# Output projection of a hybrid decoder step: column tiles 0 to 3 and 12 to 15 with tokens as rows, the sample tokens in fp32 column groups, and only block 1 finished behind the last product

## The chip, the cores and the metric

The kernel runs on one core of one Trainium2 chip. The time is the device time of one execution, in microseconds (us). The program works in fp32 throughout; large products are made of float32r pieces.

## The reference, cut to what matters

One layer of a decoder is run on 512 prompt tokens and on 8 x 4 = 32 sample tokens. The part that the change touches is the end of it:

```python
y = (jax.nn.sigmoid(g_m) * jnp.einsum('btc,cd->btd', br_m, w_proj_m)
     + jax.nn.sigmoid(g_a) * jnp.einsum('btc,cd->btd', br_a, w_proj_a))
out = jnp.einsum('btc,cd->btd', y, w_out)
return _layernorm(DN_ALPHA * x + out, ln_w, ln_b).astype(x.dtype)
```

`y` and `x` have 2048 columns, `w_out` is 2048 x 2048. The layer norm runs over the 2048 columns of each token, so no token can be finished before the last column of its row is there.

## The kernel before, in words

**Layout.** Activations lie with features on the 128 partitions and T = 544 tokens (512 prompt, 32 sample) in the free dimension: 16 tiles of 128 features (index k). A weight column tile (index ct, 128 output columns) is loaded in two halves of 8 k each (`load_half`, 512 KB, three buffers of tag "raw") and split into a float32r high part and a low rest (`split`: ScalarE casts, VectorE subtracts). Each fp32 product is made of three float32r products: high x high, high x low, low x high. In `products` the weights are held in the array and the tokens move, 272 columns at a time.

**The output projection (`wo`) has four stages.**

- *Lead*, ct 0 to 3: `gemm` with all 544 tokens as moving columns, 96 products a tile. ScalarE copies the two banks into a tile, and SyncE's queue (SP) stores it to DRAM (`d_o`). Meanwhile `operand_sums` makes the sums for the next stage from reloaded `d_y`; it is a generator that `tick()` moves on, four ticks a tile.
- *Pairs*, ct 4 to 11: `paired` makes two column tiles with seven half products instead of eight (Strassen's scheme), each 24 matmuls of 272 columns. The results are parked in `d_o` too (`end_park`). `plain_back` reloads the lead's four tiles and hands them to `add_residual`: four PE transposes turn the prompt tokens into rows, VectorE adds them to the residual rows (`z0`, `zr`), and a fifth transpose does the samples, whose rows lie in `zs` with the four column quarters on four groups of 32 partitions.
- *Last four tiles*: ct 12 is again done with all tokens moving. For ct 13 to 15 the split weights are kept (`w3`), and only tokens 256 to 543 are done that way (288 moving columns). Then `rows_of(0)` and `rows_of(1)` do blocks 0 and 1 (128 tokens each) with the tokens held and 384 weight columns moving, so their result already has tokens as rows. During these tiles `pairs_back` transposes the eight parked tiles, `load_rows` brings the residual rows, `fetch` the parked tiles and `load_ln` the norm's weights, all through SP.
- *End*: blocks 2 and 3 and the samples are normalised during the row products (`others`, `finish`, `moments`). Block 0's sum and weighting also run there (`first_rows`), but its bias is added on PE behind the last product (`scaled`, with `biases`). Block 1 follows whole: `add_rows`, statistics, four quarters `weighed` on VectorE, one quarter through PE and three `shifted` on VectorE.

**Order.** Tile's scheduler fixes each engine's order when the kernel is built, from priorities (`high_priority`) and its own estimate of durations; `issue_after` pins an instruction behind another. Each engine and each DMA queue then works its list in that order. PSUM has eight banks: four of tag "sm" (`sm()`), four of tag "bank" (`bank()`).

## Time and profile before

| | us |
|---|---|
| median of three runs | 2443.71 (2440.34 to 2447.24) |
| the profiled execution | 2442.73 |
| its span, first to last instruction | 2440.9 |
| PE busy in it | 2425.6 (99%) |
| VectorE busy | 1910.2 (78%) |
| ScalarE busy | 1252.0 (51%) |
| GpSimd busy | 533.8 (22%) |

All stages below are times from the start of the span. PE is TensorE's matmuls, PEld its weight loads, DVE VectorE, ACT ScalarE, POOL GpSimd, SPq the queue of SyncE. A matmul's own duration contains its pipeline, so prices of matmuls are read from the spacing in the chain.

### The profile page before, as it was taken

The page shows a single profiled execution, that of the slowest core. Times are in us where ns is not written, and L with a number is a line of the kernel's source. Part 1 is how long each engine was busy: PE and PEld are TensorE (multiplying, and loading weights), DVE is VectorE, ACT ScalarE, POOL GpSimd, SP SyncE. Part 2 cuts the span into 40 slices and gives each one's busy share as a digit, 9 for nine tenths or more (in the row PEclk, how much of TensorE's full clock was granted, in tenths as well). Part 3 has the DMA queues.
Part 4 walks back from the last instruction along what each step waited for, and adds up shares of the span by engine and source line. Part 5 has one row for each costly group of instructions (what it writes and reads, how often), then busy time and mean ns, then how long its engine had stood idle before and what let it go on. Part 6 is the DMA issues. An engine that isn't in the chain of part 4 may idle for free.

```text
span 2440.9 us, 49025 instructions
## 1 busy us (share of the span) xinstructions
PE 2425.6 (99%) x19394; PEld 2372.5 (97%) x19394; DVE 1910.2 (78%) x2879; ACT 1252.0 (51%) x2074; POOL 533.8 (22%) x509
## 2 busy tenths in 40 slices
PE   8999999999999999999999999999999999999998
PEld 8999999999999999999999999999999999999997
DVE  7768888888888888887877888878865676877666
ACT  6456676666666665443433444444654444434432
POOL 3114333333333431211111121120000120111111
PEclk9999999999999999999999999999999999999999
DMA  6876766667767655577687677587864588898776
GB/s 179 197 178 155 164 157 156 153 155 178 167 169 177 164 141 159 153 221 231 192 255 232 174 231 225 174 245 217 264 204 148 186 236 265 233 235 270 199 218 205
DMA packets 569597, 479.88 MB, mean 197 GB/s; under 512 B 48664, under 2 KB 464136, under 8 KB 569112
## 3 DMA queue, kind: packets, MB, share of 16 engines
q1 hardware_dynamic: 550776, 411.22, 56.9%
q0 software_dynamic: 18112, 64.76, 13.5%
q8 instruction: 152, 2.49, 0.4%
q10 hardware_dynamic: 480, 0.79, 0.1%
q14 instruction: 77, 0.63, 0.1%
HBM read 326.35 MB, written 100.77 MB: 175 GB/s over the span
## 4 chain that ended last, share of the span: by engine, by line
PE 97%; DMA 2%; DVE 1%; ACT 0%; issue 0%; SPq 0%; DVEq 0%; POOLq 0%; ACTq 0%
PE bank L699 49%; PE bank L701 24%; PE bank L218 10%; PE sm L1529 2%; PE bank L1335 1%; PE sm L1568 1%; PE sm L814 1%; PE sm L1584 1%; PE sm L865 1%; PE sm L218 1%; PE sm L2049 1%; DMA raw<-raw 1%; PE sm L840 1%; PE sm L1340 1%; DMA raw<-in_w_out 1%; DMA raw<-in_w_proj_a 0%
## 5 line engine op out<-in xcount | busy, mean ns | idle before, releaser
L208 ACT CAST wh<-raw 128x1024 fp32r<-128x1024 f32 x641 | 671.8, 1048 | 822.4 <-PE bank L699 697.1
L209 DVE TENSOR_TENSOR wl<-raw,wh 128x1024 fp32r<-128x1024 f32 x641 | 801.2, 1250 | 198.8 <-ACT wh L208 185.6
L699 PE MATMUL bank<-xk,wh 128*128 128x272 f32 x2336 | 323.4, 289 | 0.0
L679 DVE TENSOR_TENSOR raw<-raw,raw 128x1024 f32<-128x1024 f32 x244 | 310.9, 1275 | 9.7 <-DMA raw<-in_w_proj_a 2.3
L699 PEld LDWEIGHTS bank<-xk,wh 128*128 128x128 f32 x2336 | 303.4, 188 | 1.9 <-issue 1.4
L718 POOL TENSOR_TENSOR ev<-p,ev 128x272 f32<-128x272 f32 x85 | 117.7, 1384 | 453.2 <-ACT ev L717 429.7
L699 PE MATMUL bank<-n2h,wh 128*128 128x272 f32 x656 | 170.0, 291 | 0.0
L699 PE MATMUL bank<-n3h,wh 128*128 128x272 f32 x656 | 169.5, 291 | 0.3 <-ACT wh L208 0.2
L701 PE MATMUL bank<-xk,wl 128*128 128x272 f32 x1168 | 169.8, 287 | 0.0
L699 PE MATMUL bank<-s1h,wh 128*128 128x272 f32 x656 | 169.6, 291 | 0.0
L699 PE MATMUL bank<-n2l,wh 128*128 128x272 f32 x656 | 168.0, 287 | 0.0
L699 PE MATMUL bank<-n3l,wh 128*128 128x272 f32 x656 | 167.6, 288 | 0.0
L699 PE MATMUL bank<-s4h,wh 128*128 128x272 f32 x656 | 167.5, 289 | 0.0
L699 PE MATMUL bank<-s1l,wh 128*128 128x272 f32 x656 | 167.4, 287 | 0.0
L699 PE MATMUL bank<-s4l,wh 128*128 128x272 f32 x656 | 167.0, 287 | 0.0
L701 PEld LDWEIGHTS bank<-xk,wl 128*128 128x128 f32 x1168 | 155.5, 188 | 0.1
L677 POOL DMA_DIRECT2D raw<-raw x96 | 83.2, 866 | 320.3 <-DVE ev L726 209.9
L699 PE MATMUL bank<-a11h,wh 128*128 128x272 f32 x584 | 150.4, 289 | 0.0
L699 PE MATMUL bank<-a11l,wh 128*128 128x272 f32 x584 | 149.4, 288 | 0.0
L699 PEld LDWEIGHTS bank<-n3h,wh 128*128 128x128 f32 x656 | 123.4, 188 | 2.2 <-issue 1.2
L699 PEld LDWEIGHTS bank<-s1h,wh 128*128 128x128 f32 x656 | 123.2, 188 | 1.6 <-issue 1.0
L699 PEld LDWEIGHTS bank<-n2h,wh 128*128 128x128 f32 x656 | 123.4, 188 | 1.2 <-issue 1.2
(552 smaller groups left out, 5800.2 us busy)
## 6 DMA issues: line engine op xcount, KB each, us to landing
raw<-in_w_in SPq DMA_DIRECT2D x296, 512.0 KB
raw<-raw POOLq DMA_DIRECT2D x96, 512.0 KB, 5.0
C<-in_state_mlstm_C SPq DMA_DIRECT2D x32, 1024.0 KB
out<-C SPq DMA_DIRECT2D x64, 512.0 KB
raw<-in_w_proj_a SPq DMA_DIRECT2D x32, 512.0 KB
raw<-in_w_proj_m SPq DMA_DIRECT2D x32, 512.0 KB
raw<-in_w_out SPq DMA_DIRECT2D x32, 512.0 KB
d_v<-ev SPq DMA_DIRECT2D x16, 272.0 KB
```

The costliest lines, as they stand in the source:

```text
L208: state["cast"] = A.copy(wh[:, k:k + n], raw[:, k:k + n])
L209: state["split"] = V.tensor_tensor(out=wl[:, k:k + n], in0=raw[:, k:k + n], in1=r32(wh[:, k:k + n]), op=ALU.subtract)
L218: PE.matmul(ps[f][:, :w], a[:, kk], b(k, c, w), start=(k == 0 and n == 0), stop=(k == 15 and n == 2))
L677: state["summed"] = G.dma_start(out=w[out][:], in_=w[b][:], accum_op=ALU.add)
L679: V.tensor_tensor(out=w[out][:], in0=w[a][:], in1=w[b][:], op=ALU.add)
L699: PE.matmul(ps, wh[:, k], x(p, k), start=(first and k == 0 and p == 0), stop=False, skip_group_check=True)
L701: state["end"] = PE.matmul(ps, wl[:, k], x(0, k), start=False, stop=(k == 7), skip_group_check=True)
L718: G.tensor_tensor(out=c22, in0=p1, in1=c11, op=ALU.subtract)
L814: PE.matmul(pp[:, c0 + w0:c0 + 256], qs[a][:, j * 128:j * 128 + 128], kx[:, k0:k0 + 256 - w0], start=(n == 0), stop=(n == 1))
L840: PE.transpose(pt[:, b * 128:b * 128 + 128], s_[:, b, 128:256], ident)
L865: PE.matmul(po[:, b * 128:b * 128 + n], VA[:, b], p_[:, 2 * b:2 * b + n // 128], start=(b == 0 and m == 0), stop=(b == 3 and m == 1), skip ...
L1529: state["cells"] = PE.matmul(pp[:, 0:258], a[:, b * 128:b * 128 + 128], b_[:, b, f], start=(b == 0 and n == 0), stop=(b == 3 and n == 2))
```

## The change

In the lead and in the last four tiles all prompt tokens are now done with the tokens held and 512 weight columns moving. A weight load is 256 rows of `w_out` by 512 columns (`load_wide`, also 512 KB, in rows of 2 KB instead of 512 bytes), eight loads a stage. The lead's four blocks stay in the four "sm" tiles and are added to the residual rows straight from PSUM (`lead_back`): no evacuation, no parking, no transposes. In the last stage blocks 2 and 3 are done while the weights arrive; all split weights are kept, and blocks 0 and 1 follow. The sample tokens are done in plain fp32: a copy of y (`y_s32`) is held in four groups of 32 columns of the array, one k in each, and the raw weights move past. The four partial sums are added on VectorE in the lead, and by a product with a selection matrix in the last stage. Parked tiles 10 and 11 are kept in SBUF. At the end block 0 is finished entirely on VectorE during the products of block 1, block 3 through ScalarE and GpSimd's adding DMA, and block 1 with two quarters through PE.

```diff
     def back():
         for k in range(14):
             t_ = tx.tile([128, T], F32, tag="ty", name=nm("ty"))
             nc.sync.dma_start(t_[:], d_y[k])
             hilo(t_[:], yh_[k // 4][:, k % 4], yl_[k // 4][:, k % 4])
+            G.tensor_copy(y_s32[:, k], t_[:, SEQ:T])
             if k % 2:
                 yield
...
         sg = merge([p_[:, :HT] for p_ in gemm(wm, ct * 128, bmh, bml, every=4, prio=AHEAD)])
         nc.sync.dma_start(d_y[ct], sg[:])
         hilo(sg[:], yh_[ct // 4][:, ct % 4], yl_[ct // 4][:, ct % 4])
+        G.tensor_copy(y_s32[:, ct], sg[:, SEQ:T])
...
     spawn(operand_sums(d_y, Y, act3, 3))
-    for ct in range(4):
-        ps = gemm(wo, ct * 128, yh, yl, every=4, prio=AHEAD)
-        ot = ev()
-        for p_, o_ in halves(ps, ot):
-            A.copy(o_, p_)
-        nc.sync.dma_start(d_o[ct], ot[:])
...
+    def load_wide(c0, j):
+        raw = wr.tile([128, 2, 512], F32, tag="raw", name=nm("raw"))
+        state["load"] = nc.sync.dma_start(raw[:], wo[:, 2 * j:2 * j + 2, c0:c0 + 512])
+        return raw
+
+    def split_wide(raw, p, tags=(None, None)):
+        wh, wl = (p.tile([128, 2, 512], F32R, name=nm(n), **(dict(tag=t_) if t_ else {})) for n, t_ in zip(("wh", "wl"), tags))
+        with tc.high_priority(offset=AHEAD):
+            state["cast"] = A.copy(wh[:], raw[:])
+            state["split"] = V.tensor_tensor(out=wl[:], in0=raw[:], in1=r32(wh[:]), op=ALU.subtract)
+        return wh, wl
+
+    def row_products(ps, t, k, w):
+        yk = slice(t * 128, t * 128 + 128)
+        hi, lo = yh_[k // 4][:, k % 4, yk], yl_[k // 4][:, k % 4, yk]
+        for n, (a, p) in enumerate(((hi, 0), (lo, 0), (hi, 1))):
+            state["rows_end"] = PE.matmul(ps[:], a, w[p][:, k % 2], start=(k == 0 and n == 0), stop=(k == KT - 1 and n == 2))
+
+    def sample_products(ps, k0, raws):
+        for c in range(4):
+            PE.matmul(ps[c * 32:c * 32 + 32, :], y_s32[:, k0 + c], raws[c // 2][:, c % 2], start=(k0 == 0),
+                      stop=(k0 == KT - 4), tile_position=(0, c * 32))
+
+    def wide(c0, blocks, ps_s, raws, place, step):
+        for j in range(8):
+            while len(raws) < min(j + 3, 8):
+                raws.append(load_wide(c0, len(raws)))
+            step(j)
+            if j % 2 == 0:
+                sample_products(ps_s, 2 * j, raws[j:j + 2])
+            w = place(j, raws[j])
+            for k in (2 * j, 2 * j + 1):
+                for t, ps in blocks.items():
+                    row_products(ps, t, k, w)
+                tick()
+
+    lead_rows, lead_samples = {t: sm() for t in range(4)}, bank()
+    wide(0, lead_rows, lead_samples, [], lambda j, raw: split_wide(raw, wp, ("wh", "wl")), lambda j: None)
     drain()
     esT.close()
...
-    def load_ln():
-        for name in ("ln_w", "ln_b"):
-            state[name] = pk.tile([128, D], F32, tag="pk", name=nm("pk"))
-            nc.sync.dma_start(state[name][:], i[name].partition_broadcast(128))
-
...
+    def load_ln(name):
+        state[name] = pk.tile([128, D], F32, tag="pk", name=nm("pk"))
+        nc.sync.dma_start(state[name][:], i[name].partition_broadcast(128))
...
+    rows = {}

     def add_rows(t):

-        zt = zcol(D - G3 * 128, G3 * 128)[:, t]
-        V.scalar_tensor_tensor(zt, zt, ALPHA, rows[t][:, 0:G3 * 128], op0=ALU.mult, op1=ALU.add)
+        zt = zcol(D - 512, 512)[:, t]
+        V.scalar_tensor_tensor(zt, zt, ALPHA, rows[t][:], op0=ALU.mult, op1=ALU.add)
         stats(t, t + 1, 3)
         moments(t)
...
-    def rows_of(t, meanwhile):
-        ps = rows[t] = sm()
-        for k in range(KT):
-            if k == 3:
-                meanwhile()
-            yk = slice(t * 128, t * 128 + 128)
-            hi, lo = yh_[k // 4][:, k % 4, yk], yl_[k // 4][:, k % 4, yk]
-            with tc.issue_after(state["turned"].ins) if t == 0 and k == 3 else ExitStack():
-                for n, (a, p) in enumerate(((hi, 0), (hi, 1), (lo, 0))):
-                    state["rows_end"] = PE.matmul(ps[:, 0:G3 * 128], a, w3[k // 8][p][:, k % 8].rearrange("p g c -> p (g c)"),
-                              start=(k == 0 and n == 0), stop=(k == KT - 1 and n == 2))
-
...
-    def plain_back():
-
-        for ct in range(4):
-            t_ = c5t()
-            with tc.issue_after(state["load"].ins):
-                nc.sync.dma_start(t_[:], d_o[ct])
-            for _ in range(5):
-                yield
-            add_residual(ct, t_, 0, 5)
+    def lead_back():
+        for t, ps in lead_rows.items():
+            V.scalar_tensor_tensor(z0[:, t], z0[:, t], ALPHA, ps[:], op0=ALU.mult, op1=ALU.add)
+        yield
+        V.scalar_tensor_tensor(zs[0:32], zs[0:32], ALPHA, lead_samples[0:32], op0=ALU.mult, op1=ALU.add)
+        for c in range(1, 4):
+            V.tensor_tensor(out=zs[0:32], in0=zs[0:32], in1=lead_samples[c * 32:c * 32 + 32], op=ALU.add)
         yield
         stats(0, 4, 0)
...
     def pairs_back():
-        for ct in range(4, 12):
-            yield
-            add_residual(ct, parked[ct - 4], 0, 5)
-            if ct == 6:
-                with tc.issue_after(state["load"].ins):
-                    fetch(10, 12)
-            elif ct % 4 == 3:
+        for ct in (10, 11, 8, 9, 7, 4, 5, 6):
+            yield
+            add_residual(ct, parked[ct], 0, 5)
+            if ct in (9, 6):
                 yield
                 stats(0, 4, ct // 4)
-        load_ln()
+            if ct in (7, 6):
+                load_ln("ln_w" if ct == 7 else "ln_b")
+
+    parked = {}
+
+    def end_keep(o1, o2):
+        parked.update({10: o1, 11: o2})
...
     load_rows(0)
-    spawn(plain_back())
+    spawn(lead_back())
     YM = operands((yh_, yl_), Y)
-    paired([dict(wv=wo, x=YM, cA=ct * 128, cB=ct * 128 + 128, scale=1.0, acc=True, end=end_park(ct)) for ct in range(4, 12, 2)])
+    paired([dict(wv=wo, x=YM, cA=ct * 128, cB=ct * 128 + 128, scale=1.0, acc=True, end=end_park(ct) if ct < 10 else end_keep)
+            for ct in range(4, 12, 2)])
     state["end"] = None
     drain()
-    raws = [load_half(wo, ct * 128, half) for ct, half in ((12, 0), (12, 1), (13, 0))]
+    raws = [load_wide(D - 512, j) for j in range(3)]
...
     state["zr"] = d1.tile([128, 4, 1536], F32, name="zr")
-    parked = []
     with tc.issue_after(state["load"].ins):
-        load_rows(1)
-        fetch(4, 7)
-    spawn(pairs_back())
-    ps = gemm(wo, 12 * 128, yh, yl, cols=CUT, prio=AHEAD, raws=raws[:2])
-    ot = ev()
-    evac(ot, ps)
-    later = [residual_task(12, ot)]
...
-    w3 = [[wD.tile([128, 8, G3, 128], F32R, name=nm("w3")) for p in range(2)] for half in range(2)]
-    for g in range(G3):
-        ct = 16 - G3 + g
...
+        load_rows(2)
+        fetch(7, 10)
+
+    def place(j, raw):
+        kept.append(split_wide(raw, wp, ("wh", "wl")) if j < 2 else split_wide(raw, wD))
+        return kept[-1]
+
+    def step(j):
+        if j == 2:
+            spawn(pairs_back())
         with tc.issue_after(state["load"].ins):
-            if g == 0:
-                fetch(7, 10)
-                load_rows(2)
-            elif g == 1:
+            if j == 1:
+                load_rows(1)
+                fetch(4, 7)
+            elif j == 3:
                 load_rows(3)
-        if g == 1:
-            for task in later:
-                spawn(task)
-        for half, raw in enumerate(raws):
-            wh, wl = (w[:, :, g] for w in w3[half])
-            with tc.high_priority(offset=AHEAD):
-                hilo(raw[:], wh, wl)
-            products([ps], half, wh, wl, yh, yl, ((0, 256, 288),), every=4)
-        ot = ev()
-        A.copy(ot[:, 256:T], ps[:, 0:288])
-        if g == 0:
-            later.append(tail_task(ct, ot))
-        elif g < G3 - 1:
-            spawn(tail_task(ct, ot))
...
+    kept = []
+    rows.update({t: bank() for t in (2, 3)})
+    last_samples = bank()
+    wide(D - 512, dict(rows), last_samples, raws, place, step)
+
+    cm, lwq, lbq = (ev()[:, 0:512] for _ in range(3))
+    cq, ones, diag = cm[:, 0:128], cm[:, 128:256], cm[:, 256:384]
...
+    G.memset(ones, 1.0)
+    QUARTERS = [(c, c + 512) for c in range(0, D, 512)]
+
+    def samples_back():
+        part = wr.tile([128, 512], F32, tag="raw", name=nm("part"))
+        A.copy(part[:], last_samples[:])
+        pt = sm()
+        PE.matmul(pt[:NS, :], cc[:, C_SEL:C_SEL + 32], part[:], start=True, stop=True)
+        V.scalar_tensor_tensor(zs[96:128], zs[96:128], ALPHA, pt[:NS, :], op0=ALU.mult, op1=ALU.add)
+        moments(4)

     def others():
-        add_residual(15, ot, 2, 5)
-        stats(2, 4, 3)
-        for t in (2, 3, 4):
-            moments(t)
-        finish(2)
-
-    ones = cm[:, 128:256]
-    G.memset(ones, 1.0)
-    diag = {0: cm[:, 256:384], 1: cm[:, 384:512]}
-    QUARTERS = [(c, c + 512) for c in range(0, D, 512)]
-
-    def factors(t):
-        A.activation(diag[t], ident, AF.Copy, scale=mv[:, t, 2:3])
-
-    def scaled(t, q, zt):
-
-        c0, c1 = QUARTERS[q]
-        ps = biased[t, q]
-        PE.matmul(ps, diag[t], zt, start=False, stop=True)
-        copied = A.copy(zt, ps)
-        by_sync = t == 0 and q < 3
-        stored = (nc.sync if by_sync else nc.scalar).dma_start(y_p[0, t * 128:t * 128 + 128, c0:c1], zt)
-        if by_sync:
-            state["stored"] = stored
-        return copied
+        add_rows(2)
+        with tc.issue_after(state["square"].ins):
+            finish(2)
+        add_rows(3)
+        finish(3)
+
+    def rows_of(t, meanwhile):
+        rows[t] = bank()
+        for k in range(KT):
+            if t == 0 and k == 1:
+                with tc.high_priority(offset=2000):
+                    samples_back()
+                    finish_samples()
+            if k == 3:
+                meanwhile()
+            with tc.issue_after(state["turned"].ins) if t == 0 and k == 0 else ExitStack():
+                row_products(rows[t], t, k, kept[k // 2])
...
     def first_rows():
-        with tc.high_priority(offset=2000):
-            add_rows(0)
-            state["w0"] = [weighed(0, *c) for c in QUARTERS]
-            factors(0)
-        finish(4)
-        finish(3, plain=3)
...
-    rows_of(0, others)
-    rows_of(1, first_rows)
...
-    with tc.issue_after(state["rows_end"].ins), tc.high_priority(offset=5000):
-        biases([(0, q, bank()) for q in range(4)])
-    copied = [scaled(0, q, zt) for q, zt in enumerate(state["w0"])]
-    with tc.high_priority(offset=4000):
-        add_rows(1)
+        add_rows(0)
+        for c0, c1, zt in [(*c, weighed(0, *c)) for c in QUARTERS]:
+            shifted(0, c0, c1, zt)
         with tc.issue_after(state["power"].ins):
             for q in range(4):
                 G.dma_start(out=ys_rows[:, q * 512:q * 512 + 512], in_=zs[q * 32:q * 32 + 32])
+
+    rows_of(0, others)
+    rows_of(1, first_rows)
+    BY_PE = 2
+    with tc.issue_after(state["rows_end"].ins), tc.high_priority(offset=5000):
+        biased = [bank(), sm()]
+        for q in range(BY_PE):
+            r = slice(q * 32, q * 32 + 1)
+            PE.matmul(biased[q][:], ones[r], state["ln_b"][r, q * 512:q * 512 + 512], start=True, stop=False,
+                      tile_position=(q * 32, 0))
+    with tc.high_priority(offset=4000):
+        add_rows(1)
         w1 = [weighed(1, *c) for c in QUARTERS]
-        with tc.issue_after(copied[1].ins):
-            factors(1)
-        biases([(1, 0, sm())])
-        scaled(1, 0, w1[0])
-        for q in (1, 2, 3):
-            shifted(1, *QUARTERS[q], w1[q], behind=state["stored"])
+        A.activation(diag, ident, AF.Copy, scale=mv[:, 1, 2:3])
+        for q in range(BY_PE):
+            PE.matmul(biased[q][:], diag, w1[q], start=False, stop=True)
+            A.copy(w1[q], biased[q][:])
+            nc.scalar.dma_start(y_p[0, 128:256, q * 512:q * 512 + 512], w1[q])
+        for q in range(BY_PE, 4):
+            shifted(1, *QUARTERS[q], w1[q])
     drain()
```

## Rows read from the trace of the kernel before

**Rows 1.** Page, chain that ended last, whole span, by engine.

```profile
PE 97%; DMA 2%; DVE 1%; ACT 0%; issue 0%; SPq 0%; DVEq 0%; POOLq 0%; ACTq 0%
```

**Rows 2.** Windows by stage: us, busy PE, PEld, DVE, ACT, POOL, then PEclk, DMA share, GB/s.

```profile
2237.00:2284.80 47.80, 47.80 (x387) 47.80 (x386) 38.34 (x80) 22.63 (x49) 5.94 (x8) 1.00 0.81 238
2284.80:2371.35 86.55, 86.55 (x694) 86.50 (x694) 52.21 (x61) 34.89 (x43) 11.54 (x11) 1.00 0.72 185
2371.35:2409.37 38.02, 37.46 (x292) 36.39 (x292) 23.48 (x38) 7.85 (x11) 0.20 (x1) 1.00 0.80 260
2428.05:2440.90 12.85, 5.55 (x18) 2.05 (x18) 6.30 (x11) 3.20 (x6) 3.04 (x5) 0.85 0.72 223
```

**Rows 3.** Chain in order of time, output projection: start us, us, instructions.

```profile
2254.92 29.87 PE bank L218 x240
...
2284.79 2.02 PE bank L699 x16
...
2371.35 12.06 PE bank L218 x96
...
2405.93 3.44 PE sm L218 x26
...
2411.28 6.85 PE sm L2049 x39
...
2418.54 1.05 PE sm L2193 x2
```

**Rows 4.** Chain in order of time, transposes between two half products.

```profile
2302.88 0.44 PE sm L1956 x4
```

**Rows 5.** Chain in order of time, two stretches of the cells' products (L1568).

```profile
1782.40 0.69 PE sm L1568 x3
...
1785.49 2.22 PE sm L1568 x10
```

**Rows 6.** Chain, then timeline: one state update between half products.

```profile
1041.40 0.99 PE bank L1335 x8
...
1042.83 2.21 PE bank L699 x16
...
1041.34 1.06 PE L1335 MATMUL bank<-C,qz 128*32 128x512 f32 x8
```

**Rows 7.** Timeline of SP and ACT, then chain: loads in the last stage.

```profile
2369.97 0.37 SPq L195 DMA_DIRECT2D raw<-in_w_out  x1
...
2375.72 1.05 ACT L257 CAST w<-raw 128x1024 fp32r<-128x1024 f32 x1 [2.81 <-DMA raw<-in_w_out]
...
2384.03 8.68 DMA raw<-in_w_out
```

**Rows 8.** Groups by line and form, DVE, 2371.35 to 2409.37: busy us, mean ns.

```profile
L258 DVE TENSOR_TENSOR w<-raw,w 128x1024 fp32r<-128x1024 f32 x6 | 7.3, 1220 | 3.1 <-ACT w L257 3.1
L1957 DVE SCALAR_TENSOR_TENSOR zr<-zr,sm 128x512 f32<-128x512 f32 x9 | 6.2, 686 | 8.5 <-PE sm L1956 8.3
L1969 DVE BATCH_NORM_STATS2 stt<-zr 128x6 f32<-128x512 f32 x8 | 4.9, 681 | 0.1
```

**Rows 9.** Timeline of the tail: start us, us, instruction.

```profile
2428.08 0.55 DVE L2034 SCALAR_TENSOR_TENSOR zr<-zr,sm 128x384 f32<-128x384 f32 x1 [1.18 <-PE sm L2049]
2429.93 0.99 POOL L1996 TENSOR_TENSOR mv<-mv,mh 128x1 f32<-128x1 f32 x1 [3.28 <-DVE mv L1986]
...
2431.54 0.40 ACT L2163 ACTIVATE room<-cc,mv 128x128 f32<-128x128 f32 x1
...
2432.41 2.07 DVE L2011 SCALAR_TENSOR_TENSOR zr<-zr,mv,pk 128x512 f32<-128x512 f32 x3
...
2433.18 2.63 SPq L2013 DMA_DIRECT2D out<-zr  x3
```

**Rows 10.** Windows of the tail, columns as in rows 2.

```profile
2436.00:2439.40 3.40, 0.00 (x0) 0.00 (x0) 0.00 (x0) 0.00 (x0) 0.00 (x0) 0.67 0.90 339
2439.40:2440.90 1.50, 0.00 (x0) 0.00 (x0) 0.00 (x0) 0.00 (x0) 0.00 (x0) 0.50 0.01 3
```

More of the change, by code (lines that the diff above doesn't have):

```diff
@@ L1889, in _build @@
     yh, yl = whole(yh_), whole(yl_)
+    y_s32 = pool(es, "ys", 1, side="left").tile([128, KT, NS], F32, name="y_s32")
     def back():
@@ L1989, in moments @@
             V.bn_aggr(m[:, 0:2], stt[:, t, 0:1])
-            V.scalar_tensor_tensor(m[:, 1:2], m[:, 0:1], m[:, 0:1], m[:, 1:2], op0=ALU.mult, op1=ALU.add)
+            state["square"] = V.scalar_tensor_tensor(m[:, 1:2], m[:, 0:1], m[:, 0:1], m[:, 1:2], op0=ALU.mult, op1=ALU.add)
             pm = sm()
@@ L1996, in moments, with finish @@
         state["power"] = G.tensor_tensor(out=m[:, 2:3], in0=m[:, 1:2], in1=mh[:, 0:1], op=ALU.pow)
-    def finish(t, cuts=(0, 512, 1280, D), plain=0):
-        if t == 4:
-            V.scalar_tensor_tensor(zs, zs, mv[:, t, 0:1], lwq, op0=ALU.subtract, op1=ALU.mult)
-            A.activation(zs, zs, AF.Copy, scale=mv[:, t, 2:3])
-            G.dma_start(out=zs, in_=lbq, accum_op=ALU.add)
-            return
-        parts = [(c0, c1, weighed(t, c0, c1)) for c0, c1 in zip(cuts, cuts[1:])]
-        added(t, parts[plain:])
-        for part in parts[:plain]:
-            shifted(t, *part)
-    def shifted(t, c0, c1, zt, behind=None):
-        V.scalar_tensor_tensor(zt, zt, mv[:, t, 2:3], state["ln_b"][:, c0:c1], op0=ALU.mult, op1=ALU.add)
-        with tc.issue_after(behind.ins) if behind else ExitStack():
-            nc.sync.dma_start(y_p[0, t * 128:t * 128 + 128, c0:c1], zt)
-    def weighed(t, c0, c1):
-        zt = zcol(c0, c1 - c0)[:, t]
-        V.scalar_tensor_tensor(zt, zt, mv[:, t, 0:1], state["ln_w"][:, c0:c1], op0=ALU.subtract, op1=ALU.mult)
-        return zt
-    def added(t, parts):
+    def finish(t, cuts=(0, 512, 1280, D)):
+        parts = [(c0, c1, weighed(t, c0, c1)) for c0, c1 in zip(cuts, cuts[1:])]
         for c0, c1, zt in parts:
@@ L2025, in added, with finish_samples, shifted, weighed @@
             nc.sync.dma_start(y_p[0, t * 128:t * 128 + 128, c0:c1], zt)
[L2027 to L2029 removed]
+    def finish_samples():
+        V.scalar_tensor_tensor(zs, zs, mv[:, 4, 0:1], lwq, op0=ALU.subtract, op1=ALU.mult)
+        A.activation(zs, zs, AF.Copy, scale=mv[:, 4, 2:3])
+        G.dma_start(out=zs, in_=lbq, accum_op=ALU.add)
+    def shifted(t, c0, c1, zt):
+        V.scalar_tensor_tensor(zt, zt, mv[:, t, 2:3], state["ln_b"][:, c0:c1], op0=ALU.mult, op1=ALU.add)
+        nc.sync.dma_start(y_p[0, t * 128:t * 128 + 128, c0:c1], zt)
+    def weighed(t, c0, c1):
+        zt = zcol(c0, c1 - c0)[:, t]
+        V.scalar_tensor_tensor(zt, zt, mv[:, t, 0:1], state["ln_w"][:, c0:c1], op0=ALU.subtract, op1=ALU.mult)
+        return zt
+    rows = {}
     def add_rows(t):
[L2033 to L2034 removed]
+        zt = zcol(D - 512, 512)[:, t]
+        V.scalar_tensor_tensor(zt, zt, ALPHA, rows[t][:], op0=ALU.mult, op1=ALU.add)
         stats(t, t + 1, 3)
         moments(t)
[L2038 to L2052 removed]
     def end_park(ct):
@@ L2177, in first_rows @@
-    def first_rows():
-        with tc.high_priority(offset=2000):
-            add_rows(0)
-            state["w0"] = [weighed(0, *c) for c in QUARTERS]
-            factors(0)
-        finish(4)
-        finish(3, plain=3)
-    rows_of(0, others)
-    rows_of(1, first_rows)
-    biased = {}
-    def biases(which):
-        for g, (t, q, ps) in enumerate(which):
-            c0, c1 = QUARTERS[q]
-            biased[t, q], r = ps[:], slice(g * 32, g * 32 + 1)
-            PE.matmul(biased[t, q], ones[r], state["ln_b"][r, c0:c1], start=True, stop=False, tile_position=(g * 32, 0))
```

22 lines of the change are left out of this document (1 added, 21 removed).

## Prediction

> **What bounds the kernel now.** I read the chain of waits first. TensorE (PE) carries 97% of it [rows 1], so a microsecond taken out of PE's stream, or out of what follows its last product, is a microsecond of the span; work removed from the other engines is worth nothing by itself. Next I cut the end of the trace into the stages that the change touches [rows 2]: the lead of the output projection (column tiles 0 to 3) up to 2284.80, its paired tiles 4 to 11 up to 2371.35, the products of tiles 12 to 15 up to 2428.05, where the last row product ends, and a tail of 12.85 us to the end. In the first two stages PE has no idle time at all. In the third it has 0.56 us (37.46 of 38.02). Only in the tail is it not the bound: there the chain runs through VectorE (DVE) and then the stores [rows 9, 10]. The granted clock is 1.00 through all products, the upper of its two levels (2.4 GHz), and falls only in the tail. So each stage is a sum of instructions at their spacing, taken from the chain [rows 3].
>
> **Prices on PE.** A product with 272 moving columns costs 29.87/240 = 0.1245 us in the lead and 12.06/96 = 0.1256 in tile 12; one with 288 costs 3.44/26 = 0.1323; one with 384 costs 6.85/39 = 0.1756 [rows 3]. Four transposes of 128x128 cost 0.44 [rows 4], so a tile's five 0.55. The new form is 512 columns wide, in float32r. The trace has it in the mLSTM cells (L1568), which make twelve of 512 columns and then twelve of 384 [rows 5]: the first three cost 0.69, so 0.230 each; of the next ten, 2.22 in all, nine are 512 wide and one 384, so (2.22 - 0.18)/9 = 0.227. I take 0.229.
>
> The sample products are fp32, four at a time, each on its own 32 columns of the array. The state update at L1335 has that shape (128x32 held, 128x512 moving, four column positions): eight instructions cost 0.99 us [rows 6]. So the four run beside each other. What the return to the full array costs is not shown for them. Behind the row-tiled four at L1340, which follow, the next 16 products took 2.21 us, where such 16 take 2.02 [rows 3, 6]; so 0 to 0.19 more, and a group is worth 0.99 to 1.18. I take 1.09, the middle, since a row position is near to a column position but not the same.
>
> The Trainium skill speaks against the groups here: "TensorEngine Tiling (Array Packing)", Key Properties, says that a change of tiling mode drains TensorE. By that rule each group pays the upper end, eight of them 0.7 us more than in my sum; without a drain they pay 0.8 us less. The 0.19 above agrees with the rule, but no row shows it behind a column group.
>
> **Lead.** Removed: 4 x 96 = 384 products of 272, 384 x 0.1245 = 47.8 us. Added: 16 k x 4 blocks x 3 = 192 products of 512, 44.0 us, and 4 sample groups, 4.4 us. Sum +0.5 us, bounds -0.2 (0.227 and 0.99) and +1.1 (0.230 and 1.18). That it is no gain is the point: 128 fewer columns per (k, product) are paid back by the fp32 groups. The eight weight loads and splits stay, as do 16 ticks, so the operand sums keep their pace. The eight evacuations on ScalarE, four parking stores and reloads vanish off the path. The GpSimd copies of 32 columns (16 of them) stand beside a queue busy 5.94 of 47.80 us [rows 2]: nothing.
>
> **Pairs.** The four parked lead tiles are no longer transposed: 4 x 0.55 = -2.2 us, all on PE's stream, which has no gap there. In their place DVE adds four PSUM tiles into the residual at about the 0.69 us that such an add of 512 columns takes [rows 8], and four additions of 32 rows, on an engine busy 52 of 86.55 us: nothing. The lead's four PSUM tiles and the samples' bank are held until the first residual rows arrive; the pairs use none of the four, and of their own four banks only the other three in the first seven half products (21 us).
>
> **Last four tiles.** Before: 96 products of 272 (12.1), 144 of 288 (19.1), 96 of 384 (16.9), 54 transposes (40 for parked tiles, 5 for tile 12, 9 for tiles 13 to 15: 5.9), one bias product (1.05) and a small one (0.1): 55.1 of the 56.70 us. The 1.6 left are the 0.56 idle and changes between kinds of product. After: 192 of 512 (44.0), 4 sample groups (4.4), 40 transposes (4.4), one fp32 product of 512 that adds the four sample groups (1.05, like the bias product), the small one (0.1): 53.9. Of the 1.6 I leave half, for there are fewer kinds but more changes: 54.7, so -2.0 us. Bounds without a stall: -2.8 and -1.2.
>
> Here the cover is thin. Weights come in three buffers of 512 KB, and buffers j and j+1 are now held until the sample group of the even step j has read them. The next group needs two later buffers. Between two groups PE has 24 products (5.5), a group and, from step 2 on, four residuals (2.2): 8.8 us, of which a load may take some 7.7. Before, such loads behind the residual rows landed after up to 8.68 us; one issued at 2369.97 was there by 2375.72, 5.75 us later [rows 7]. All transfers together ran at a share of 0.80 there [rows 2]. The bytes hardly change; the time for them shrinks from 38.0 to about 31 us (22.0 + 4.4 + 4.4, and the first row products). I cost this at nothing because 5.75 fits, and put 8.68 into a rival. On SP the moved row loads and fetches stand ahead of weight loads 4 and 6, so these are what would come late. DVE has six splits of 1.22, eight residuals of 0.69 with a small one each for the samples, and eight statistics of 0.68: some 20 of these 31 us [rows 8].
>
> **Tail.** Before, DVE starts at 2428.08 with block 1, then statistics, four weighed quarters and three shifted ones, done at 2434.48; SP's last issue ends at 2435.81 [rows 9]. Block 0's megabyte leaves in the same time through the same 16 engines: their share is still 0.90 from 2436.0 to 2439.4, and 1.5 us more pass to the end [rows 10]. After, only block 1 is behind the last product: add 0.69, statistics and moments 1.2 (pow began 1.85 behind the start of an add of 0.55), four weighed quarters 2.7 and two shifted 1.3 at a third of 2.07 each: DVE done 6.0 us behind the product, stores issued by 6.6 at the latest (moments done at 1.9, then pow 0.99 and factors 0.40 with their hand-overs to 3.4, two fp32 products to 5.4, the second copy behind the first store's issue to 6.2, issue 0.39), 1 MB instead of 2. At 339 GB/s [rows 10] a megabyte takes 3.1 us; counted from the first store at 5.3 that is 8.4, and the last store, issued at 6.6, takes more: at most the 3.6 from 2435.81 to 2439.4, which had another megabyte in the way, and I take 2.3: 8.9. With 1.5 the tail is 10.4, so -2.4 us. Bounds: -3.0 if the first store decides, 0 if block 0 spills over.
>
> Block 0 is covered by the 48 products of block 1, 11.0 us; it needs 1.7 + 2.7 + 2.7 = 7.1 of DVE. But DVE also has blocks 2 and 3 (4.4 each), the samples (2.9) and the last residuals (3.5) in the 23 us between the wide products and the end: 22.3 in all. It fits with under a microsecond to spare.
>
> **Sum.** +0.5 - 2.2 - 2.0 - 2.4 = -6.1 us on a span of 2440.9, so 2434.8. The profiled execution took 2442.73, 1.0 under the median of 2443.71; taken off the median: 2437.6 us.
>
> **Rivals.**
> 1. *Every bound falls well.* -0.2 - 2.2 - 2.8 - 3.0 = -8.2: 2435.5 us. For it: the four sample products side by side in [rows 6]. Against: the return cost there. Chance 0.32, faster.
> 2. *A cover is lost*, so part of the change doesn't do what it says: block 0 isn't ready when the last product ends, and its shifted quarters queue on DVE before or among block 1's (tail gain 0: -3.7, 2440.0 us), or the weight loads land after 8.68 us and three groups wait 1.0 us each (-3.1, 2440.6 us). Chance 0.18, within the bound.
> 3. *The last stage starves and the kernel is slower.* Place: the sample groups of steps 2, 4 and 6, behind loads 3, 5 and 7, which queue behind residual rows in the in-order queue of SP. Above a landing time of 7.7 + 6.1/3 = 9.7 us the whole gain is gone, and above 7.7 + 13.4/3 = 12.2 us the kernel is 7.3 us slower: 2451 us. For it: 8.68 us is not far away [rows 7], and in the new order the residual rows stand nearer to the loads. Against: wide rows make a quarter as many pieces of a weight load. Chance 0.10.
>
> **How the numbers follow.** The forecast case has 0.40. About 0.3% of the time, 7.3 us, is what a measurement can tell from no change; the three runs shown lie 6.9 us apart. The forecast of -6.1 stays within it, rival 1 goes beyond, rival 2 stays within: faster 0.32, same 0.58, slower 0.10. The range goes from 1.5 us under rival 1 (2434.0), for the scatter of a median, to a little past no gain (2444.5), leaving out rival 3 and the far end of rival 1.
>
> **What would show it.** Right: lead of about 48.3 us with four groups of 8 instructions at 1.0 to 1.2; pairs of 84.4 without transposes; last stage of 54 to 55.5; tail of 10 to 11 with one block in it. Wrong: PE idle before sample groups with a weight load as releaser; groups split in two and two; a sum into block 1 that waits on DVE; 512-column products well off 0.229.

## The result and the profile after

The changed kernel takes 2448.48 us (median of 14 runs, 2446.42 to 2451.31) against 2441.68 us before (14 runs): a ratio of 1.0027, 95% interval 1.0020 to 1.0034. It is slower, by just under the 0.3% that was set as the bound, where -6.1 us had been forecast. The profiled span is 2448.0 us (before 2440.9).

The windows by stage of the kernel after, with the columns of [rows 2]: lead, pairs, the last four tiles in two pieces (blocks 2 and 3, then blocks 0 and 1), tail.

```profile
2236.82:2286.32 49.50, 49.50 (x226) 36.56 (x226) 37.35 (x79) 21.44 (x43) 7.61 (x11) 1.00 0.75 233
2286.32:2375.84 89.52, 85.33 (x677) 84.59 (x679) 55.25 (x62) 34.62 (x41) 13.24 (x12) 1.00 0.65 164
2375.84:2412.59 36.75, 36.75 (x173) 23.16 (x173) 21.38 (x33) 6.96 (x8) 0.00 (x0) 1.00 0.68 232
2412.59:2435.40 22.81, 22.81 (x97) 17.65 (x97) 17.41 (x34) 5.69 (x7) 8.83 (x11) 1.00 0.72 155
2435.40:2448.00 12.60, 4.95 (x9) 1.47 (x8) 5.77 (x10) 1.57 (x3) 2.69 (x5) 0.63 0.78 270
```

Against before [rows 2] the lead is 1.7 us longer, the pairs 3.0, the last four tiles 2.9 (59.56 against 56.70), and the tail 0.25 shorter: +7.3, all of it ahead of the last product (the lead starts 0.2 us earlier in this profile, so the spans differ by 7.1). Forecast were +0.5, -2.2, -2.0 and -2.4. Ahead of the last product only the pairs have PE idle: 4.2 us of 89.52. Its waits there, by releaser (us in total, times, longest):

```profile
PE bank L701 <- DVE wl L209: 2.9, 1, 2.9
PE bank L699 <- ACT wh L208: 1.3, 1, 1.3
```

Both wait for split weights: L209 makes the low part on DVE, L208 the high part on ScalarE from a sum that DVE makes (L679). DVE's timeline at the start of the pairs says why they are late:

```profile
2288.16 0.68 DVE L2061 SCALAR_TENSOR_TENSOR zs<-zs,bank 32x512 f32<-32x512 f32 x1 [5.12 <-DMA zs<-in_x_sample]
2288.76 1.21 DVE L679 TENSOR_TENSOR raw<-raw,raw 128x1024 f32<-128x1024 f32 x1
2290.00 0.68 DVE L2063 TENSOR_TENSOR zs<-zs,bank 32x512 f32<-32x512 f32 x1
2290.71 1.28 DVE L2059 SCALAR_TENSOR_TENSOR z<-z,sm 128x512 f32<-128x512 f32 x2
...
2295.14 1.21 DVE L209 TENSOR_TENSOR wl<-raw,wh 128x1024 fp32r<-128x1024 f32 x1
```

The addition of the lead's sample bank stands in DVE's list ahead of weight sums (L679) and splits (L209). It waits 5.12 us for the samples' residual rows, whose load goes out behind a megabyte of other rows. DVE is idle meanwhile, and the sum comes at 2288.76. Then the lead's other additions and their statistics stand in the way as well: the high part was cast at 2290.08, in 1.05 us, but its low part, which PE needs, is split only at 2295.14. So the wait and the work behind it are late together.

In the last four tiles PE never waits, but the chain in order of time shows the sample groups (L1939) in pieces; a product in fp32 has two records (64 for the 32 products), so x8 is a whole group of four and x2 is one product:

```profile
2375.84 0.99 PE bank L1939 x8
...
2377.97 0.97 PE bank L1939 x2
...
2381.94 0.97 PE bank L1939 x2
...
2386.66 0.98 PE bank L1939 x4
...
2393.37 0.98 PE bank L1939 x4
...
2395.98 0.98 PE bank L1939 x4
...
2409.10 3.49 PE bank L1935 x15
```

With the two halves of the last group (not shown, the same lengths) there are eight sittings where four were costed, and one product alone takes 0.97 us, as long as four together. The last row gives the price of a 512-column product with nothing between: 3.49/15 = 0.233 us.

In the tail, SP's timeline (queue, start us, us, line, operation):

```profile
2428.70 6.18 SPq L2026 DMA_DIRECT2D out<-zr  x3
2434.97 1.20 SPq L2035 DMA_DIRECT2D out<-z  x1
2436.26 5.53 SPq L2035 DMA_DIRECT2D out<-zr  x5
```

and what SP's queue waited for from 2410 on, by releaser (us in total, times, longest; the 12.7 us end at 2422.30, before block 0 had anything to store):

```profile
SPq L2026 <- DMA z<-pk: 13.9, 2, 12.7
SPq L2026 <- DMA zr<-pk: 9.1, 4, 2.7
```

DVE's timeline, the end of block 0 and the start of block 1:

```profile
2429.80 2.07 DVE L2034 SCALAR_TENSOR_TENSOR zr<-zr,mv,pk 128x512 f32<-128x512 f32 x3
2435.55 0.69 DVE L2047 SCALAR_TENSOR_TENSOR zr<-zr,bank 128x512 f32<-128x512 f32 x1 [3.68 <-PE bank L1935]
```

Block 0 is finished on DVE from 2429.13 to 2431.87, in good time, yet its first store (L2035) is issued at 2434.97. In front of it stand the stores of blocks 2 and 3 (L2026), which wait for GpSimd's adding transfers of the bias (z<-pk, zr<-pk). Before, block 3's bias was added by DVE; the change gives it to adding transfers as well: 2.62 MB of GpSimd's transfers in the last 33 us, where the end of the kernel before has 1.57 MB. A piece of 384 KB lands after 8.4 us (median) in place of 5.1.

The chain of the tail shows one more thing that was not costed. Block 1's two quarters through PE are fp32 products of 512 columns, and here they take 2.07 and 1.72 us; the bias product in [rows 3], right behind other products, took 1.05. The windows of these products, after and before (PE busy in the second column, granted clock third from the end):

```profile
2440.30:2444.20 3.90, 3.78 (x4) 1.17 (x4) 1.12 (x2) 0.63 (x2) 0.00 (x0) 0.50 0.91 330
2429.00:2433.60 4.60, 4.60 (x14) 1.82 (x10) 4.53 (x9) 2.61 (x5) 3.04 (x5) 1.00 0.64 148
```

After, PE had stood idle for 3.77 us ahead of them, and the granted clock is 0.50, the lower level (1.2 GHz). Before, the products of block 0 and of block 1's one quarter followed the last row product, PE had no idle time there, and the clock was 1.00.

### The profile page after: what moved, and what is told of

The parts are those of the page before. It is cut to its first block, busy times and chain, and to the rows that moved or that the text cites. A ratio compares the mean times of both kernels' runs of the same rounds, so it can differ in the third digit from the quotient of the medians.

```text
span 2448.0 us, 48375 instructions
## 1 busy us (share of the span) xinstructions
PE 2428.1 (99%) x19078; PEld 2344.5 (96%) x19078; DVE 1910.9 (78%) x2874; ACT 1249.1 (51%) x2061; POOL 544.7 (22%) x528
## 5 line engine op out<-in xcount | busy, mean ns | idle before, releaser
L208 ACT CAST wh<-raw 128x1024 fp32r<-128x1024 f32 x631 | 661.1, 1048 | 817.7 <-PE bank L699 673.6
L209 DVE TENSOR_TENSOR wl<-raw,wh 128x1024 fp32r<-128x1024 f32 x631 | 791.2, 1255 | 194.6 <-ACT wh L208 180.9
L679 DVE TENSOR_TENSOR raw<-raw,raw 128x1024 f32<-128x1024 f32 x244 | 309.5, 1269 | 13.9 <-DMA raw<-in_w_in 4.4
L699 PEld LDWEIGHTS bank<-s1l,wh 128*128 128x128 f32 x656 | 123.7, 189 | 1.1 <-DVE s1l L258 0.9
```

What stands on the lines that cost most here:

```text
L208: state["cast"] = A.copy(wh[:, k:k + n], raw[:, k:k + n])
L209: state["split"] = V.tensor_tensor(out=wl[:, k:k + n], in0=raw[:, k:k + n], in1=r32(wh[:, k:k + n]), op=ALU.subtract)
L679: V.tensor_tensor(out=w[out][:], in0=w[a][:], in1=w[b][:], op=ALU.add)
L699: PE.matmul(ps, wh[:, k], x(p, k), start=(first and k == 0 and p == 0), stop=False, skip_group_check=True)
```

## The experiments

Each ratio is to the kernel before on the same chip. A difference to the changed kernel is between medians that are not all from one chip, and known to some 2 us; so where an edit acts is read from the stages of its profile. Three edits first, each alone and then together.

**e1: the samples' stores moved behind block 1's power.** In the trace after, GpSimd's power for block 1 starts at 2439.20, behind four stores that waited 8.67 us for the samples' adding transfer.

```
             shifted(0, c0, c1, zt)
-        with tc.issue_after(state["power"].ins):
-            for q in range(4): G.dma_start(out=ys_rows[...], in_=zs[...])
...
         add_rows(1)
+        (the same stores here)
```

> Edit: only the four stores of the sample rows move, from behind block 0's pow to behind block 1's pow, as in the kernel before. Theory A (GpSimd's queue): in the changed kernel block 1's pow stood behind these stores, which waited for the adding DMA into the sample rows to land; pow began 3.9 us behind the last product instead of 1.9, and its factors, products and stores came 2 us late. Then the tail falls from 12.5 to 10.4 to 11 us and the time by 1.5 to 2 us, to about 2446.5. Rival B (stores): the tail is set by the megabyte of block 0 that is still leaving through the DMA engines; then pow comes earlier but the tail stays at 12 to 12.5 us and the time does not move. Lead, pairs and last stage stay as they are under both.

2448.41 us, ratio 1.0029 (1.0018 to 1.0040). The power came at 2438.49, the last copy's store was issued at 2443.16 in place of 2444.77 (with a last product 0.9 us later), and the time and the tail, 12.5 us, stayed: block 1's chain does not set the end by itself. Theory A fell, rival B fits.

**e2: the lead's additions later.**

```
     def lead_back():
+        for _ in range(3):
+            yield
```

> Edit: the task that adds the lead's result to the residual rows begins three ticks (three half products, 9 us) later; nothing else. Theory A (VectorE's queue): the sample add stood first in VectorE's list and waited 5.1 us for the sample rows' load, and the weight sum and split for the pairs stood behind it. Then the pairs fall from 89.5 us to 84.3 to 85, PE waits there vanish, and the time falls by 4.5 to 5.2 us, to about 2443.5. Rival B (the pairs' own loads): the weights of the first pair landed late because buffers of the lead were held by the sample groups; then PE still waits 3 to 5 us at the start of the pairs, with a load or an adding DMA as releaser, and the time moves by less than 1.5 us.

2448.73 us, 1.0028 (1.0019 to 1.0038). A miss of the edit, not of the theory: the schedule still put the samples' addition in front, and DVE waited 6.50 us for the same load. e7 repeats it with a pin.

**e3: every sample group whole.** The four products are chained, at a higher priority.

```
+        last = None
-        for c in range(4):
-            PE.matmul(...)
+        for c in (2, 3, 0, 1):
+            with tc.high_priority(offset=3000), tc.issue_after(last.ins) if last else ExitStack():
+                last = PE.matmul(...)
```

> Edit: the four sample products of a group are issued in the order 2, 3, 0, 1, each pinned behind the one before and at high priority, so that the group begins only when its second weight buffer is there and stays in one piece; nothing is left out. Theory A (split groups): in the last stage three of the four groups were issued in two or three parts, nine... eight sittings of about 1.17 us instead of four; whole, the last stage falls by 4 x 1.17 = 4.7 us, to about 55, and the time to about 2444. Rival B (late weights): the parts cost what they cost because PE would have had to wait for the second buffer anyway; then PE shows idle time before the groups, with a weight load as releaser, of 3 us or more, and the time moves by less than 1.5 us.

2448.91 us, 1.0028 (1.0017 to 1.0039). The groups are whole and the last product ends at 2429.6, 5.8 us earlier (1.6 of it from a lead that ends earlier in this profile), yet the tail takes most of it. Its window in e3:

```profile
2429.60:2446.30 16.70, 4.71 (x9) 1.48 (x8) 5.77 (x10) 1.58 (x4) 3.95 (x6) 0.70 0.77 245
```

**e4: the three together.**

> Edit: the three edits together. If the three causes are separate, their gains add: 2 + 5 + 4.7 = 11.7 us under the changed kernel's 2448.5, so about 2437, some 4.5 to 5 us (0.2%) under the kernel before. If one hides another (an earlier pairs stage that meets later loads), the sum is short by 2 us or more, about 2439 to 2441.

2450.42 us, 1.0035 (1.0023 to 1.0048), tail 16 us. My theory that the end follows the last product fell here. What was left was the path of the stores, and the next four take it apart.

**e5: block 3's bias back on DVE.**

```
         add_rows(3)
-        finish(3)
+        for c0, c1, zt in [(*c, weighed(3, *c)) for c in QUARTERS]:
+            shifted(3, c0, c1, zt)
```

> Block 3's shift (factor and bias) goes back to VectorE, in four parts of 512, as the kernel before had it; its three adding transfers of GpSimd (1 MB) are gone. Everything else is the changed kernel. Theory S (the store queue: block 3's stores wait for adding transfers and hold all stores behind them on SyncE's queue): block 3's stores leave at about 2431, block 0's first store at about 2433 instead of 2434.97, SyncE's wait of 6.18 us for block 3's rows is gone, and the tail behind the last product falls from 12.6 to about 10.5 us: 2446 us, ratio to before about 1.0018. VectorE pays 2.8 us more, which its idle 3.68 us ahead of block 1's last product covers. Rival V (VectorE becomes late: block 1's residual starts behind block 0's shift): the tail stays at 12 us or more, 2448 us. Rival P (the products set the end): no change, 2448.5.

2446.13 us, 1.0018 (1.0010 to 1.0027): -2.35 us against the changed kernel. The stores of block 3 leave from 2423.91 on, block 0's first at 2430.75, and the tail is 11.3 us, 1.3 less than after. Rival V fell: block 1's addition starts right behind its product.

**e6: block 3 left with the adding transfers, its stores behind block 0's.** 

```
         for c0, c1, zt in parts:        (in finish: for t == 3 the parts are kept in late, without a store)
...
             shifted(0, c0, c1, zt)
+        with tc.issue_after(state["stored"].ins):        (block 0's last store)
+            for c0, c1, zt in late:
+                nc.sync.dma_start(y_p[0, 3 * 128:4 * 128, c0:c1], zt)
```

> Block 3 is still finished by GpSimd's adding transfers, but its three stores stand behind block 0's four on SyncE's queue instead of ahead of them: the same bytes, another order. Theory S (a held queue): block 0's first store is issued at about 2431 to 2432 instead of 2434.97, the tail falls by 1.5 to 2.5 us, 2446 to 2447. Rival B (the bytes: the 16 DMA engines have so much to move behind the last loads, adding transfers above all, that the order doesn't matter): block 0's stores leave early, but the last stores land no earlier, 2448 to 2449. Rival P (the products set the end): 2448.5.

2445.97 us, 1.0018 (1.0009 to 1.0026): -2.5 us with the same bytes and the same engines' work. SP's timeline in e6 (L2040 is the store of `shifted`, L2173 block 3's):

```profile
2427.49 1.23 SPq L2040 DMA_DIRECT2D out<-z  x1
2428.80 3.81 SPq L2040 DMA_DIRECT2D out<-zr  x3
2432.71 1.20 SPq L2173 DMA_DIRECT2D out<-z  x1
```

Block 0 leaves 7.5 us earlier than after (last product 3.1 us earlier in this profile). The tails of e5 and e6, to be held against 12.60 after:

```profile
2435.40:2446.70 11.30, 5.04 (x9) 1.48 (x8) 5.77 (x10) 1.57 (x3) 1.59 (x3) 0.63 0.47 162
2432.30:2444.20 11.90, 4.99 (x9) 1.47 (x8) 5.77 (x10) 1.57 (x3) 3.00 (x5) 0.61 0.83 291
```

So the order in SP's queue, held by a store that waits, was worth 0.7 us of the tail, and the order together with the adding transfers that e5 takes out 1.3. The rest of both medians' gain is not shown to come from the edits: in e6's profile the lead ends 1.7 us earlier, and PE waits for 1.7 us at the start of the pairs, where it waited 4.2 after, in code that is the same.

**e7: the lead's additions pinned behind the splits.**

```
     def lead_back():
+        yield
         for t, ps in lead_rows.items():
-            V.scalar_tensor_tensor(z0[:, t], ...)
+            with tc.issue_after(state["split"].ins): V.scalar_tensor_tensor(z0[:, t], ...)
...  (the first addition of the samples likewise)
```

> The additions of the first 512 columns' banks (rows and samples) are pinned on VectorE behind the weight splits made so far; nothing else differs. Theory Q (VectorE's queue: the samples' addition waits 5.12 us for its load with the pairs' splits behind it): the two waits of TensorE at the start of the pairs (2.9 us for a low part and 1.3 for a high part) go, the pairs take about 86 instead of 89.5 us, and since all that follows moves with them the time falls by 2.5 to 3.5 us: 2445 to 2446. Rival L (GpSimd's adding sum of the weights is late on its own, behind its own transfers): the wait for the high part stays, 2447. Rival B (the end is set by transfers that don't start earlier): the last product comes 3 us earlier and the tail grows by as much, 2448.5.

2443.86 us, 1.0006 (0.9997 to 1.0015): -4.6 us, more than theory Q asked for. Stage windows of e7 (pairs, last four tiles, tail):

```profile
2286.50:2371.60 85.10, 84.96 (x678) 84.54 (x680) 54.07 (x62) 34.84 (x41) 11.75 (x12) 1.00 0.67 172
2371.60:2431.00 59.40, 59.40 (x268) 40.71 (x260) 38.76 (x66) 12.56 (x14) 8.84 (x11) 1.00 0.71 201
2431.00:2443.70 12.70, 5.02 (x9) 1.48 (x8) 5.77 (x10) 1.57 (x3) 2.74 (x5) 0.73 0.78 268
```

The pairs lose 4.4 us and their idle time, and the tail does not grow: pairs and everything behind them move together. Rival L fell, for no wait for the high part is left. Rival B fell here: the transfers start earlier with the products of blocks 2 and 3.

**e10: e1, e3, e5 and e7 together.**

> Four edits together: block 3 on VectorE, every group of four sample products kept whole, the samples' stores behind the last power, and the additions of the first columns pinned behind the splits. If theories S and Q hold and the groups are worth their 4.8 us once the tail no longer waits: pairs 86, last stage about 54.5 (4.8 less), tail about 10.5: 2448.5 - 3.3 - 4.8 - 2 = 2438.4, below the kernel before. Rival B (the end is set by the bytes behind the last loads): the products end 8 us earlier and the tail grows to 17 us or more, 2446 to 2449, as in the three edits together before. Between: the transfers of the last stage (loads of the rows and weights, DMA share over 0.9) come late, and TensorE waits for them, 2441 to 2444.

2442.03 us, 1.0001 (0.9993 to 1.0010): as fast as before, 3.6 us above the sum. The last product ends at 2424.2, and the tail is 14.9 us. DVE is busy for 18.96 of the last 19.2 us ahead of it and comes to block 2 only at 2415.2, so its adding transfers run into the end again.

**e11, e12: e5 with e7; e6 with e7.**

> Two edits: block 3 on VectorE and the first columns' additions pinned behind the splits; the sample groups stay split and the samples' stores stay where the change has them. Alone they gave -2.3 and -4.6 us against the changed kernel. Theory A (the two lie on different stretches and add up): 2448.5 - 6.9 = 2441.5 us, the time of before. Rival T (both are paid out of the same stretch, the stores at the end): no better than the better one, 2443.9. If A holds, the four edits together at 2442.0 say that whole groups and later sample stores brought nothing on top.

> Two edits: block 3 stays with GpSimd's adding transfers, its stores stand behind block 0's, and the first columns' additions are pinned behind the splits. Theory A (they add up): 2448.5 - 2.5 - 4.6 = 2441.4 us. Rival T (one stretch pays for both): 2443.9.

2442.57 us, 1.0005 (0.9996 to 1.0015), and 2443.11 us, 1.0007 (0.9999 to 1.0016). By the ratio to before neither can be told from e7 alone (1.0006), where 1.0000 would have been the sum: inconclusive between theory A and rival T. The stages decide it. Pairs and tail of e11, then of e12:

```profile
2290.30:2375.40 85.10, 84.96 (x678) 84.54 (x680) 54.05 (x62) 34.84 (x41) 11.65 (x12) 1.00 0.67 172
2434.80:2446.10 11.30, 4.99 (x9) 1.47 (x8) 5.77 (x10) 1.57 (x3) 1.44 (x2) 0.61 0.47 161
2285.75:2370.85 85.10, 84.97 (x678) 84.55 (x680) 54.04 (x62) 34.83 (x41) 11.73 (x12) 1.00 0.66 166
2430.30:2442.10 11.80, 4.81 (x9) 1.47 (x8) 5.77 (x10) 1.57 (x3) 3.04 (x5) 0.80 0.84 293
```

The pairs are those of e7 and the tails those of e5 and e6: both gains are there in full, and the tail's 0.7 to 1.3 us is too little for the medians to show. Rival T fell.

**e13: e12 with whole groups and the samples' stores later.**

> As the two edits (block 3's stores behind block 0's, additions pinned), with every sample group kept whole and the samples' stores behind the last power. Against block 3 on VectorE with the same three edits this takes 2.8 us off VectorE, which was busy for 18.96 of the 19.2 us ahead of the last product there. Theory V (VectorE was what kept the gain of the whole groups): the samples' chain and block 2's adding transfers come earlier, the tail falls from 14.9 to 11 to 12.5 us behind a last product at about 2424.5, 2437 to 2439.5 us, faster than before. Rival B (the bytes: about 5.3 MB of stores and adding transfers behind the last load, with the DMA engines full): the tail stays near 15 us, 2441 to 2442.

2442.75 us, 1.0006 (0.9997 to 1.0014). Theory V falls: with less on DVE nothing is gained, and the tail is 15.1 us. From 2415 to 2435 the DMA share is 0.99 to 1.08 in each 5 us, so by these shares the transfers themselves are the bound (rival B); 2.62 MB of them are GpSimd's, against 1.57 in e10.

**e14: e10 with DVE's work in another order.** Block 2 first, then the samples' moments, then block 3. The lines are shown against the changed kernel; e10's other edits are in it too.

```
         add_rows(2)
-        with tc.issue_after(state["square"].ins):
-            finish(2)
         add_rows(3)
-        finish(3)
+        finish(2)
+        with tc.issue_after(state["square"].ins):
+            w3 = [(*c, weighed(3, *c)) for c in QUARTERS]
+        for c0, c1, zt in w3:
+            shifted(3, c0, c1, zt)
```

> As the four edits together (block 3 on VectorE, whole groups, samples' stores behind the last power, additions pinned), in another order on VectorE: block 2 is weighed first, so that its adding transfers (1 MB) start about 6 us earlier, at about 2411 in place of 2417, where the DMA engines were a third to half busy; then the samples' moments; then block 3. Nothing is left out or added. Theory B (with the products out of the way the end is set by how early the slow adding transfers are over, then by the plain stores): SyncE's queue is free for blocks 3 and 0 by about 2419 instead of 2425, the samples' adding transfer starts at about 2421 instead of 2427.89, and block 1's last store, issued at about 2432.7, ends the kernel: tail 11.5 to 12.5 us behind a last product at about 2424.5, 2438 to 2440 us by the median, ratio 0.999 or below. Rival V (VectorE's own sum of work ahead of block 1's last product sets the end whatever its order): 2441 to 2442, as before.

2438.52 us, ratio 0.9986 (0.9977 to 0.9995): faster than both kernels, 10 us under the change as it was made. Windows of e14 by stage, then two stretches of its end:

```profile
2236.10:2284.40 48.30, 48.30 (x218) 36.29 (x217) 37.15 (x78) 20.57 (x42) 7.03 (x9) 1.00 0.68 200
2284.40:2370.30 85.90, 85.76 (x681) 84.55 (x680) 54.01 (x61) 34.52 (x41) 11.65 (x12) 1.00 0.71 187
2370.30:2425.20 54.90, 54.03 (x263) 40.21 (x261) 40.77 (x71) 10.44 (x12) 7.33 (x8) 1.00 0.69 216
2425.20:2436.70 11.50, 4.90 (x9) 1.47 (x8) 6.24 (x11) 1.57 (x3) 3.02 (x5) 0.60 0.67 217
...
2410.00:2415.00 5.00, 5.00 (x24) 4.04 (x23) 4.93 (x9) 2.04 (x3) 3.72 (x4) 1.00 0.51 88
...
2425.00:2430.00 5.00, 2.18 (x7) 0.80 (x6) 4.90 (x10) 0.40 (x1) 2.34 (x4) 0.76 0.84 260
```

(Its priority moves one sample group of each stage into the stage ahead, so the windows of the lead and of the last four tiles each lack one group of 1.2 us; the pairs' window has one that belongs behind it.) The same bytes move as in e10, but the DMA engines begin earlier and are no longer full at the end (share 0.51 from 2410 to 2415 and 0.84 from 2425 to 2430, where e10 has 0.32 and 0.97): the adding transfers are issued from 2411.17, not 2417.06, and SP's queue is free for block 3 at 2419.12.

## Why the prediction was wrong

The forecast case failed at four steps; the time, 2448.48 us, came out above the range of 2434.0 to 2444.5.

1. **Pairs, "In their place DVE adds four PSUM tiles ... nothing".** I costed DVE's busy time (52 of 86.55 us) and not its order. An in-order engine can be half idle and still be late: one addition that waited for a load held the sum for the next split for 5 us, and the additions behind it held the split itself. The removal itself was right: with the additions behind the splits the pairs take 85.1 us (e7), 1.45 under before, with 0.14 us idle; 84.4 were forecast. The order was worth 4.6 us of time by the medians.
2. **Last four tiles, four groups at 1.09.** The price was 0.1 low, as is shown below; the count was wrong: the groups fell apart into eight sittings, the case that I had named as a sign of being wrong and had given no price. Whole, the stage takes 56.1 us in e14 (54.9 and the group that stands in the pairs), 0.9 of it a wait for a load, where the sum had 54.7. In time this was hidden until the tail could follow: nothing in e3.
3. **Tail.** "0 if block 0 spills over" looked at DVE, which was in time. The step that is missing from the sum is `finish(3)`, whose bias moved from DVE to GpSimd's adding transfers: one megabyte more of them, and SP's in-order queue held by the stores that wait. e5 takes 1.3 us off the tail and e6 0.7. In e5 and e14 the tail is 11.3 and 11.5 us where 10.4 were forecast, and a second term of the sum is behind that: "two fp32 products to 5.4" counts 2.0 us for them, and at the granted clock of 0.50 they take 3.8 in e14 too, on the chain that ends last. In e14 the last store is issued 8.7 us behind the last product, 2.1 later than costed, and the end comes 2.8 us behind it, 1.0 sooner. No run keeps PE busy ahead of these products, so what the full clock would give back is not shown. Block 0 itself was covered by block 1's products, as forecast.
4. **Price of the 512-column product, 0.229 us.** It is 0.233. On 192 products that is 0.8 us in the lead and 0.8 in the last stage. The 272-column price scaled by columns, 0.1245 x 512/272 = 0.234 [rows 3], would have been nearer than the short stretches of [rows 5].

A sample group costs the upper end. In e7's chain, two successive pieces of the lead show it:

```profile
2238.16 11.39 PE sm L1935 x48
2250.55 11.40 PE sm L1935 x48
```

They start 12.39 us apart; 48 x 0.233 = 11.2, so a group is worth 1.2 (1.09 taken, bounds 0.99 to 1.18): the lead is 44.7 + 4.8 = 49.5, measured 49.50. The Trainium skill's rule that a change of tiling mode drains TensorE ("TensorEngine Tiling (Array Packing)", Key Properties) stood for the upper end, and the trace agrees: 0.20 us behind each group. The Trainium skill's "TensorE: Matmul & The Clock Gate", Back-to-back issue gap, gives an isolated gap of about 216 ns for 512 columns and 131 ns sustained; this kernel's 233 ns, in float32r, lies above both, and the measurement decides.

Of the rivals, 3 (the last stage starves) did not happen: PE has no idle time there, so loads in three buffers were in time with the split groups. With whole groups, PE waits 0.87 us in e14's last stage: the cover is as thin as it was said to be. In rival 1 the lead's lower bound should be -0.3, not -0.2 (192 x 0.227 + 4 x 0.99 - 47.8); nothing hangs on it. Rival 2 named a lost cover, but the wrong ones. No case had a store that waits on SP, nor a DVE wait in the pairs. With the order mended, e14 comes near the sum without reaching it: its stages, with the moved groups counted back, are 49.5, 84.7, 56.1 and 11.5 us where 48.3, 84.4, 54.7 and 10.4 were forecast, and it is 3.2 us faster than before (0.14%), about half of the 6.1 us forecast.

What stays open: why PE's wait at the start of the pairs differs between executions of the same code there (1.7 us in e6, 4.2 after), and how much of the long tails of e3, e4, e10 and e13 is the bytes; that full DMA engines make them was read from the shares and not tried by itself.

## What to carry to other kernels

For each in-order queue (an engine's or SP's), don't ask only how busy it is: ask which instruction in it waits for a transfer, and what stands behind. A residual addition behind a late load, or a store behind a slow transfer, costs its wait to all that follows, and a pin or another order gives it back for nothing. When the stages ahead get shorter and the end doesn't move, look for the transfers that fill the DMA engines there, and start the slowest ones first. And price an instruction that follows a wait of TensorE by a row that follows one too: block 1's two fp32 products cost 3.8 us behind 3.77 us of idle time, where 2.0 had been counted.

## What the runs showed of the hardware

- One fp32 product of 128x32 on 128x512, alone on a quarter of the array's columns, takes 0.97 us, and four side by side take 0.99; each sitting costs the row products about 0.20 us more behind it (four take 1.13 us there, 0.93 elsewhere).
- Adding transfers fill the DMA engines at half the rate. In e14's stretch from 2405 to 2440 (40 slices; share in tenths, then GB/s) the DMA engines are full from slice 9 on, counted from 0; up to slice 14 block 2's adding transfers are under way and they move 160 to 210 GB/s, and in slices 15 to 20, with the plain stores, 370 to 400:

```profile
DMA  0000000039999999999991599992467993400000
GB/s 0 0 19 0 0 0 0 0 61 197 162 200 190 207 190 380 397 399 369 393 379 73 122 260 265 384 386 82 98 127 236 382 356 129 171 0 0 0 0 0
```
